# A row maximum that skips NaN: the last 34 tiles divided anew

## The chip, the cores and the metric

The kernel runs on one core of a Trainium2 chip. The metric is the device time of one execution in microseconds. A profile is one such execution, recorded by the hardware profiler; its own times count from the program's first instruction.

## The reference

```python
batch, seq, dim = 32, 2048, 2048
x = np.random.randn(batch, seq, dim).astype(np.float32)
x[np.random.rand(batch, seq, dim) < 0.1] = np.nan
...
return np.nanmax(x, axis=-1).astype(np.float32)
```

There are 65,536 rows of 2048 numbers, 537 MB, a tenth of them NaN. Of each row the largest number that isn't NaN is wanted; a row with nothing but NaN gives NaN.

## The kernel before, in words

**The tiles.** The rows lie on 128 partitions, 512 rows to each. The list `TILES` cuts them into 74 tiles, numbered here from 1. Its unit is the quarter: a quarter of a row, 512 elements of each partition. A tile of 28 quarters is seven rows of each partition, 7168 KB. An entry of `TILES` has three lists, each with the same sum:

- the loads: `[28]` is one DMA, `[20, 8]` are two;
- the pieces in which the tile is cleaned;
- the reductions: `[16, 12]` are four rows and then three.

**Cleaning a piece.** A NaN would spoil a maximum, so only the upper 16 bits of each number are treated. ACT (ScalarE) reads them and writes a "key" into a key buffer, with an activation whose two slopes send NaN to a low value (L222, `kt<-xt`). Then the key goes back, turned round, in place of the upper 16 bits. GpSimd does that (POOL, L232, `xt<-kt`) for a positive number in the list of pieces, and ACT does it (a "write-back", L222, `xt<-kt`) for a negative one. A tuple is one key operation whose parts go back separately, so `(9, -3)` is a key of 12 quarters of which GpSimd returns 9 and ACT 3. A write-back by ACT stands directly behind its key operation; one written as a float, `-3.0`, stands behind the next key operation. Then VectorE (DVE) takes the maximum over whole rows (L239).

**Buffers and order.** There are three tile buffers (`xt`), each 28 quarters, and three key buffers (`kt`), each 12. A tile's loads wait until the reductions of the tile three before it are done (L316). Loads are issued by SyncE (SP), in order. `Order` writes down all instructions and gives each the semaphore waits that it needs; every engine takes its own in the order in which they were written.

A key operation that doesn't fit into the rest of its key buffer goes to the next one and waits until what that one held has been returned. The last key operation of a tile waits for the buffer after that as well:

```python
if used + c > KEYS:
    key = (key + 1) % NKEYS
    used = 0
    kold, kfree[key] = last(kfree[key]), []
    ...
    if at + c == sum(loads) * Q:
        kold = kold + last(kfree[(key + 1) % NKEYS])
```

**Pairs.** Where a reduction needs one piece from GpSimd and one from ACT, and no other reduction needs either, `joints` makes them a pair: both count up one semaphore, and all who wait for either wait for both. That holds for the key buffers too: in `cleaned`, the event `e` with which a half's key buffer comes free is that of the pair.

```python
for a, b, k, back, when in both:
    kfree[k].append((back, when, e))
    clean.append((a, b, e))
```

`joints` leaves ACT's half out where GpSimd's piece belongs to a later step than the write-back. Tiles 70 to 73 (`APART`) have no pairs.

**The end.** Rows without a number are turned into NaN by a pass over the results (L245, twice, and L260 with L274 for one group on GpSimd), and six stores bring the results out (L461). The last store is issued when the last pass is done.

Of the kernel before, what the change touches and what calls it, by code (L numbers as in the profile page):

```python
# [23 lines left out]
    + [([28], [7, 9, 12], [16, 12])] * 7  # L24
    + [([28], [9, 12, -7], [8, 20])]
    + [([28], [7, 9, 12], [16, 12])] * 7
    + [([28], [9, 12, -7], [8, 20])]
    + [([28], [7, 9, 12], [16, 12])] * 7
    + [([28], [6, 10, 12], [16, 12])] * 3
    + [([28], [7, 9, 12], [16, 12])]  # L30
    + [([28], [6, 10, 12], [16, 12])] * 3
    + [([28], [7, 9, 12], [12, 16])] * 2
    + [([28], [7, 10, 11], [12, 16])]
    + [([28], [6, 10, 12], [16, 12])] * 3
    + [([28], [8, 11, 9], [8, 8, 12])]
    + [([20, 8], [11, -6, 6, 5], [16, 12])]
    + [([20, 8], [12, (-4, 7), 5], [8, 8, 12])]
    + [([17, 11], [12, (-4, 6), 6], [4, 12, 12])]
    + [([16, 12], [11, -5, 5, 7], [16, 12])]
    + [([13, 15], [9, -4, 7, 8], [12, 8, 8])]  # L40
    + [([14, 14], [9, -4, 4, 4, 7], [12, 8, 8])]
    + [([11, 10, 7], [5, 6, (-3, 7), 7], [4, 4, 4, 8, 8])]
    + [([11, 9, 8], [4, 7, (-2, 7), 6, -2], [4, 4, 4, 8, 8])]
    + [([8, 7, 6, 7], [3, 5, 7, (3, -3), 3, 4], [8, 4, 8, 8])]
    + [([6, 5, 6, 5, 6], [5, (5, -1), (-1, 5), 5, 3, 3], [4, 4, 4, 4, 4, 4, 4])]
    + [([5, 6, 5, 4, 4, 3, 1], [(-2, 3), 3, 3, (4, -1), 4, 4, -2.0, 2], [4, 4, 3, 1, 4, 4, 4, 4])]
    + [([4, 4, 3, 2, 4, 2, 3, 3, 3], [2, 2, 4, (-2.0, 1), 2, 3, 3, (-1, 2), (1, -1, 1), 2, -1.0], [4, 4, 4, 4, 4, 4, 4])]
)

GROUPS = [TILES[i : i + 15] for i in range(0, 60, 15)] + [TILES[60:73], TILES[73:]]  # L50
# [453 lines left out]
```

## Time and profile before

| | |
|---|---|
| median of 3 executions | 1252.54 us (1252.48 to 1253.04) |
| the profiled execution | 1252.48 us |
| its span | 1250.7 us |
| VectorE busy | 1111.4 us, 89% |
| ScalarE busy | 965.6 us, 77% |
| GpSimd busy | 1168.5 us, 93% |
| DMA, mean rate | 430 GB/s |

A line of the profile names the source line, the engine, the operation, what is written and read with partitions x elements, and how often; behind the bar are the busy time in us, the mean of one in ns, and the idle time before it with what ended it. "ACT kt L222" are key operations, "POOL xt L232" GpSimd's returns, "DVE acc L239" the reductions. In a timeline a line has its start and length in us, and a merged one counts its instructions (x3) and has the shape of the first.

### The profile page before, as it was taken

To read this page: it belongs to the slowest core of one execution; us is meant where nothing else is said; L and a number is where in the kernel's file an instruction comes from. 1 tells how busy PE (TensorE), PEld (TensorE's weight loads), DVE (VectorE), ACT (ScalarE), POOL (GpSimd) and SP (SyncE) were. 2 spreads that over 40 slices of the span, in tenths; PEclk is the share of its full clock that TensorE was granted. 3 is DMA by queue.
4 is the path that set the end of the run, shared out by engine and by line. 5 is a ranking of instruction groups with operands and counts; after the bars stand their busy time and mean duration, and the time that the engine had idled before them with its cause. 6 is when DMAs were issued, how large, how long until landed. Compare 5 with 4: busy or idle time off the path is not lost.

```text
span 1250.7 us, 891 instructions
## 1 busy us (share of the span) xinstructions
DVE 1111.4 (89%) x179; ACT 965.6 (77%) x273; POOL 1168.5 (93%) x242
## 2 busy tenths in 40 slices
DVE  0888989888889888898988888998888899999999
ACT  3777887778777877788777877777777778999997
POOL 2999989998999899998999899999999999989998
DMA  9999999999999999999999999999999999999997
GB/s 415 440 418 433 440 440 438 413 440 440 440 433 418 440 440 438 429 424 440 440 436 424 431 440 438 436 424 433 440 438 435 422 436 436 425 434 429 431 428 301
DMA packets 15991, 537.20 MB, mean 430 GB/s; under 512 B 2544, under 2 KB 2544, under 8 KB 3568
## 3 DMA queue, kind: packets, MB, share of 16 engines
q1 hardware_dynamic: 15984, 537.14, 99.4%
q14 instruction: 7, 0.06, 0.0%
HBM read 536.87 MB, written 0.26 MB: 429 GB/s over the span
## 4 chain that ended last, share of the span: by engine, by line
DMA 40%; DVE 29%; POOL 22%; ACT 9%; issue 1%; SPq 0%
DMA xt<-in_x_dram 40%; DVE acc L239 29%; POOL xt L232 22%; ACT kt L222 8%; ACT xt L222 1%; SPq L316 0%; DVE acc L245 0%; SPq L499 0%; SPq L215 0%
## 5 line engine op out<-in xcount | busy, mean ns | idle before, releaser
L232 POOL TENSOR_SCALAR xt<-kt 128x3584 int16<-128x3584 uint16 (+11 forms) x236 | 1167.4, 4947 | 77.6 <-ACT kt L222 63.9
L239 DVE TENSOR_REDUCE acc<-xt 128x3 f32<-128x6144 f32 (+4 forms) x175 | 1107.5, 6379 | 135.6 <-POOL xt L232 128.1
L222 ACT ACTIVATE kt<-xt 128x3584 uint16<-128x3584 int16 (+9 forms) x247 | 913.4, 3734 | 278.0 <-DMA xt<-in_x_dram 257.9
L222 ACT ACTIVATE xt<-kt 128x512 int16<-128x512 uint16 (+6 forms) x24 | 52.8, 2202 | 0.7
L245 DVE SCALAR_TENSOR_TENSOR acc<-acc 128x414 f32<-128x414 f32 (+1 forms) x2 | 2.2, 1111 | 0.1
L222 ACT ACT_TABLE_LOAD x1 | 1.3, 1283 | 0.9 <-SPq L215 0.9
L239 DVE TENSOR_REDUCE xt<-xt 128x1 f32<-128x1536 f32 x1 | 1.7, 1743 | 0.0
L278 DVE MEMSET scalars<- 128x1 f32 x1 | 0.1, 59 | 1.0 <-SPq L215 1.0
L260 POOL TENSOR_SCALAR late<-acc 128x91 int32<-128x91 f32 x1 | 0.5, 549 | 0.1
L274 POOL TENSOR_TENSOR acc<-acc,late 128x91 int32<-128x91 int32 x1 | 0.3, 341 | 0.1
L485 POOL MEMSET const-float32-0.0<- 128x1 f32 x1 | 0.1, 98 | 0.2 <-issue 0.2
L222 ACT ACTIVATE scalars<-scalars 128x1 f32<-128x1 f32 x1 | 0.2, 203 | 0.0
L485 POOL MEMSET const-bfloat16-1.0<- 128x1 bf16 x1 | 0.1, 101 | 0.0
L485 POOL MEMSET const-uint8-127<- 128x1 uint8 x1 | 0.1, 101 | 0.0
L485 POOL MEMSET const-float32-1.0<- 128x1 f32 x1 | 0.1, 98 | 0.0
## 6 DMA issues: line engine op xcount, KB each, us to landing
xt<-in_x_dram SPq DMA_DIRECT2D x61, 7168.0 KB, 22.6
xt<-in_x_dram SPq DMA_DIRECT2D x2, 5120.0 KB, 17.4
xt<-in_x_dram SPq DMA_DIRECT2D x3, 2816.0 KB, 22.7
xt<-in_x_dram SPq DMA_DIRECT2D x4, 2048.0 KB, 22.3
xt<-in_x_dram SPq DMA_DIRECT2D x5, 1536.0 KB, 29.1
xt<-in_x_dram SPq DMA_DIRECT2D x2, 3584.0 KB, 24.8
xt<-in_x_dram SPq DMA_DIRECT2D x6, 1024.0 KB, 26.8
xt<-in_x_dram SPq DMA_DIRECT2D x3, 1792.0 KB, 30.1
```

What stands on the lines that cost most here:

```text
L222: lambda: nc.scalar.activation(**kw),
L232: lambda: nc.gpsimd.tensor_scalar(**kw),
L239: return order.add("dve", nc.vector, lambda: do(**kw), deps)
L245: lambda: nc.vector.scalar_tensor_tensor(out=acc, in0=acc, scalar=LEAST, in1=acc, op0=ALU.is_ge, op1=ALU.mult,),
L260: lambda: nc.gpsimd.tensor_scalar(out=none, in0=acc, scalar1=LEAST, scalar2=float(0x00400000), op0=ALU.is_lt, op1=ALU.mult,),
L274: lambda: nc.gpsimd.tensor_tensor(out=bits, in0=bits, in1=none, op=ALU.add),
L278: e_warm = order.add("dve", nc.vector, lambda: nc.vector.memset(warm, 1.0), [])
L485: nc = _bacc.Bacc("TRN2", target_bir_lowering=False, num_devices=1)
```

## The change

Only `TILES` is changed, from the 41st entry on; tiles 53 and 61 stay as they were. In tiles 41 to 60 each tile is still one load, three pieces and two reductions, with other sizes, and ACT's one write-back among them, the 7 quarters of tile 41, goes to GpSimd. From tile 62 on, loads, pieces and reductions are cut otherwise. In all there are 116 loads (105 before), 246 key operations (247), 23 write-backs by ACT with 80 quarters (24 with 84), 241 returns by GpSimd (236) and 177 reductions of tiles (176).

```diff
-    + [([28], [9, 12, -7], [8, 20])]
-    + [([28], [7, 9, 12], [16, 12])] * 7
-    + [([28], [6, 10, 12], [16, 12])] * 3
-    + [([28], [7, 9, 12], [16, 12])]
-    + [([28], [6, 10, 12], [16, 12])] * 3
-    + [([28], [7, 9, 12], [12, 16])] * 2
+    + [([28], [8, 9, 11], [16, 12])]
+    + [([28], [7, 11, 10], [16, 12])]
+    + [([28], [8, 9, 11], [12, 16])]
+    + [([28], [9, 8, 11], [12, 16])] * 2
...
+    + [([28], [8, 9, 11], [12, 16])]
+    + [([28], [6, 11, 11], [16, 12])]
     + [([28], [7, 10, 11], [12, 16])]
-    + [([28], [6, 10, 12], [16, 12])] * 3
-    + [([28], [8, 11, 9], [8, 8, 12])]
-    + [([20, 8], [11, -6, 6, 5], [16, 12])]
-    + [([20, 8], [12, (-4, 7), 5], [8, 8, 12])]
-    + [([17, 11], [12, (-4, 6), 6], [4, 12, 12])]
-    + [([16, 12], [11, -5, 5, 7], [16, 12])]
-    + [([13, 15], [9, -4, 7, 8], [12, 8, 8])]
-    + [([14, 14], [9, -4, 4, 4, 7], [12, 8, 8])]
-    + [([11, 10, 7], [5, 6, (-3, 7), 7], [4, 4, 4, 8, 8])]
-    + [([11, 9, 8], [4, 7, (-2, 7), 6, -2], [4, 4, 4, 8, 8])]
-    + [([8, 7, 6, 7], [3, 5, 7, (3, -3), 3, 4], [8, 4, 8, 8])]
-    + [([6, 5, 6, 5, 6], [5, (5, -1), (-1, 5), 5, 3, 3], [4, 4, 4, 4, 4, 4, 4])]
-    + [([5, 6, 5, 4, 4, 3, 1], [(-2, 3), 3, 3, (4, -1), 4, 4, -2.0, 2], [4, 4, 3, 1, 4, 4, 4, 4])]
-    + [([4, 4, 3, 2, 4, 2, 3, 3, 3], [2, 2, 4, (-2.0, 1), 2, 3, 3, (-1, 2), (1, -1, 1), 2, -1.0], [4, 4, 4, 4, 4, 4, 4])]
+    + [([28], [6, 10, 12], [16, 12])]
+    + [([28], [8, (5, -7.0), 8], [12, 16])]
+    + [([28], [5, 7, 9, 7], [12, 8, 8])]
+    + [([20, 8], [(7, -5.0), 8, 8], [12, 8, 8])]
+    + [([15, 13], [(9, -3.0), 8, 8], [8, 8, 12])]
+    + [([13, 15], [(9, -3), 8, 8], [8, 12, 8])]
+    + [([15, 13], [10, -4, 6, 8], [12, 8, 8])]
+    + [([14, 14], [9, (-3, 2), 7, 7], [12, 8, 8])]
+    + [([11, 6, 11], [(6, -5.0), (3, 3), 4, 7], [4, 8, 8, 8])]
+    + [([9, 9, 10], [(7, -2), (6, -3), 3, 2, 5], [8, 8, 4, 8])]
+    + [([8, 7, 6, 7], [7, -1, 7, (3, -3), 3, 4], [8, 4, 8, 8])]
+    + [([7, 4, 6, 4, 7], [5, (5, -1), (2, 4), (-3, 1), 2, 3, 2], [4, 4, 4, 8, 4, 4])]
+    + [([5, 6, 5, 1, 1, 1, 2, 1, 1, 1, 1, 1, 1, 1], [(-1, 4), 3, 3, (-1, 4), 3, 4, 3, -2.0], [4, 4, 4, 4, 3, 1, 3, 1, 4])]
+    + [([4, 4, 3, 2, 2, 1, 1, 2, 2, 1, 2, 1, 1, 2], [2, 2, 4, 3, -2, 1, 2, 3, (1, 2), (-1, 2), (-2, 1)], [4, 4, 4, 4, 3, 1, 2, 2, 4])]
```

The last minus line and the last plus line are tile 74, and each line above it is one tile earlier, up to tile 61 (`[6, 10, 12]`). In the new tile 65, `[(9, -3.0), 8, 8]` with `[8, 8, 12]`, the second reduction covers quarters 8 to 16: the end of GpSimd's 9, ACT's 3 and the start of GpSimd's first 8.

## The prediction

> **What bounds the kernel now.** I read the busy shares first, then DMA and VectorE (DVE) by stretches of time, then DVE's timeline, and last ACT's and POOL's where the changed tiles begin. Tiles are counted from 1, and a quarter is 512 elements of a partition.
>
> ```profile
> span 1250.7 us, 891 instructions
> DVE 1111.4 (89%) x179; ACT 965.6 (77%) x273; POOL 1168.5 (93%) x242
> 850.00:1000.00 150.00, 134.62 (x18) 111.57 (x27) 146.72 (x27) 1.00 1.00 434
> 1050.00:1100.00 50.00, 49.84 (x10) 47.61 (x15) 47.90 (x11) 1.00 1.01 435
> 1100.00:1150.00 50.00, 49.88 (x9) 47.53 (x18) 43.70 (x11) 1.00 1.00 431
> 1150.00:1200.00 50.00, 50.00 (x16) 45.53 (x20) 48.76 (x16) 1.00 1.00 430
> 1200.00:1251.00 51.00, 48.04 (x24) 42.67 (x33) 43.86 (x26) 1.00 0.84 348
> ```
>
> The stretches give DVE, ACT and POOL busy time, clock, DMA share and GB/s. DMA is full until the last stretch: a tile of 28 quarters takes 16.9 us of it, whatever the engines do. DVE needs about 15.2 us for such a tile, so up to 1000 us it waits (134.62 of 150 busy). After 1050 us it doesn't: 49.84, 49.88 and 50.00 of 50. There a second bound stands beside DMA: DVE has a fixed amount of reducing left and no idle time in which to make good a stop.
>
> ```profile
> 1017.40 15.15 DVE L239 TENSOR_REDUCE acc<-xt 128x4 f32<-128x8192 f32 x2 [1.74 <-POOL xt L232]
> 1034.56 23.79 DVE L239 TENSOR_REDUCE acc<-xt 128x4 f32<-128x8192 f32 x4
> 1058.51 60.52 DVE L239 TENSOR_REDUCE acc<-xt 128x3 f32<-128x6144 f32 x10 [0.16 <-POOL xt L232]
> 1065.07 45.38 DVE acc L239 x8
> 1247.94 0.17 DVE acc L245
> ```
>
> Three lines are DVE's timeline, two the chain that ended last. DVE's last wait of any size ends at 1017.40 (tile 60). The chain's eight reductions from 1065.07 end at 1110.46, and the eighth is the last of tile 65: 12 quarters, 6.54 us, begun at 1103.92. From there to the end of the reductions at 1247.94 are 144.0 us, the time to which the change is compared.
>
> ```profile
> 1038.03 19.98 ACT L222 ACTIVATE kt<-xt 128x4096 uint16<-128x4096 int16 x5 [4.48 <-DMA xt<-in_x_dram]
> 1065.06 7.55 ACT L222 ACTIVATE kt<-xt 128x2560 uint16<-128x2560 int16 x2 [0.79 <-POOL xt L232]
> 1072.70 14.44 POOL L232 TENSOR_SCALAR xt<-kt 128x6144 int16<-128x6144 uint16 x3 [0.83 <-ACT kt L222]
> ```
>
> At 1038.03 ACT starts tile 62 as its load lands; earlier waits of this kind end at 1004.26 and 1021.14, so the bytes of tile 63 are there at 1038.03 + 16.9 = 1054.93. The other two lines show, small, what I expect large. The last key operation of tile 63 waits 0.79 us for POOL, because a tile's last key asks for the next key buffer as well, and a buffer whose pieces are a "pair" comes free only when both halves are done. POOL then runs dry for 0.83 us. DVE didn't feel it: pieces lay ready for it.
>
> **The change part by part.** Durations are the means by shape.
>
> ```profile
> L232 POOL TENSOR_SCALAR xt<-kt 128x4608 int16<-128x4608 uint16 x53 | 282.8, 5335 | 9.1 <-ACT kt L222 5.4
> L232 POOL TENSOR_SCALAR xt<-kt 128x3584 int16<-128x3584 uint16 x55 | 230.7, 4194 | 44.5 <-ACT kt L222 43.1
> L232 POOL TENSOR_SCALAR xt<-kt 128x2560 int16<-128x2560 uint16 x9 | 27.4, 3049 | 2.1 <-ACT kt L222 1.6
> L232 POOL TENSOR_SCALAR xt<-kt 128x4096 int16<-128x4096 uint16 x2 | 9.5, 4762 | 0.3 <-ACT kt L222 0.2
> L222 ACT ACTIVATE kt<-xt 128x4096 uint16<-128x4096 int16 x2 | 7.2, 3609 | 4.5 <-DMA xt<-in_x_dram 4.5
> L222 ACT ACTIVATE kt<-xt 128x2560 uint16<-128x2560 int16 x10 | 23.2, 2325 | 1.3 <-POOL xt L232 0.8 <-DMA xt<-in_x_dram 0.5
> ```
>
> *Tiles 41 to 60.* ACT's one write-back of 7 quarters (4.20 us) becomes POOL's. POOL's share of a tile is then 4.19 + 5.34 + 7.04 + 3 x 0.08 = 16.81 us of 16.9, so a backlog is worked off by 0.1 us a tile. Carried through POOL's pieces, tile 60's first reduction starts near 1018.2, 0.8 us later than now. The bounds are 0 and 4.2; I take 0.8. It sets only how late DVE comes to the next step, not the end.
>
> *Tile 65, the step that decides.* Its pieces are now (9, -3.0), 8, 8 with reductions of 8, 8 and 12. The second reduction needs ACT's -3 and POOL's first 8, so `joints` makes these two a pair, and the key buffer that holds the -3 is free only when POOL has done that 8. The tile's last key waits for this buffer. So it stands on ACT until POOL has written all it has been given, and POOL has nothing meanwhile. In tile 63 of before POOL still had a piece in hand.
>
> The time: tile 63 lands at 1054.93; ACT's first key (5 quarters) ends at 1057.28, POOL starts at 1057.35 and then has 5, 7, 9, 7 (tile 63), 7, 8, 8 (tile 64), 9, 8 (tile 65) in a row: 3.05 + 4.19 + 5.34 + 4.19 + 4.19 + 4.76 + 4.76 + 5.34 + 4.76 = 40.58, eight handovers of 0.08, and 0.1 where ACT's key for tile 65 is late: 41.32, to 1098.67. Then the waiting key, 0.02 + 3.61, to 1102.30; POOL's last 8, 0.07 + 4.76, to 1107.13; DVE starts the last reduction of tile 65 at 1107.15. Now it starts at 1103.92: 3.23 us later. ACT waits 4.3 us (its write-back of 3 quarters is done near 1094.3), POOL 3.7. Queued behind the key on ACT are the keys of tile 66, for which POOL waits too.
>
> DVE itself: the reductions of tiles 61 to 64 are the same, and tile 65's are 8, 8, 12 for 4, 12, 12, which sums the same. With its 0.8 us it would be ready near 1104.4, so 2.7 us of the stop show as idle.
>
> *Reducing left.* In tiles 66 to 74, 44 reductions become 45: sixteen of 8 quarters (4.41), three of 12 (6.54), eighteen of 4 (2.28), three of 1536 elements (1.74), three of 513 (0.69), two near 1024 (1.2, between the last two): 140.8 us, against 140.7. With tile 65's last 6.54, less 0.08 of overlap at 41 handovers, plus 0.02 at the four that wait for DVE's own result: 144.0 us, as now. ACT and POOL stay ahead of it: in the tail POOL finishes each piece some 2.8 us before DVE asks for it. There are two thin places, the reductions near 1118 and 1129, with 0.1 us to spare; their bounds are 0 and 0.3 us, and I take 0.
>
> *Eleven more loads* (105 to 116): one fewer in tile 63, seven more in 73, five in 74. SP issues one in 0.43 us by the chain; the stores stand behind them on SP, which is free at the latest when the last load lands, and the last store is due near 1251.4. Between 1150 and 1200 eleven loads land, between 850 and 1000 three in 50 us; the rate goes from 434 to 430 GB/s, 0.46 us in 50 for eight more, about 0.05 us a load: the last landing, at 1242.2 in the trace's DMA records, comes 0.5 us later (bounds 0 and 0.1 us a load). It is hidden: everything behind the stop has 2.7 us more between landing and reduction. Without the stop it would show.
>
> The Trainium skill speaks against this part: DMA: Bandwidth & Descriptors, section Rules for kernel authors, asks for 1 MiB or more per DMA and for coalescing small transfers. Its section on the anatomy of one DMA has a fixed part of about 2.0 us each (for the GpSimd path), by which eleven would cost 22 us, an estimate from that page.
>
> *The sum.* 1107.15 + 144.0 = 1251.15; the flagging pass and the last store as now (1250.7 - 1247.94 = 2.76) give a span of 1253.9, 3.2 more. The profiled execution took 1252.48, its span and 1.78 around it, and the median is 0.06 above that: 1253.9 + 1.84 = 1255.8.
>
> **The rivals.** *The stop doesn't reach DVE* (12%). In tile 63 of before the same kind of wait cost DVE nothing. It would do so here if DVE came to tile 65's last piece 2.7 us later, or POOL 2.7 us earlier, than I have it. DVE is then 0.5 us behind before: 1253.0, not measurably slower. Against it: POOL's row of nine pieces starts from a landing, and their durations spread by hundredths. Parts of the stop would give 1253 to 1255.
>
> *Loads that pay one by one* (5%). The stores that met an empty queue took this from issue to landing:
>
> ```profile
> out_dram<-acc SPq DMA_DIRECT2D x1, 3.5 KB, 1.4
> ```
>
> If each added load held the stream for 1.4 us, the last landing would come 15.4 later and the end with it: 1268. From 2.7 us in all (0.25 us a load) it would begin to show. Against it: 430 GB/s while those eleven landed in 50 us. By the rule on small transfers the time would go this way; the trace doesn't agree so far, with 0.05 us for a load.
>
> *Faster* (2%). The smaller last pieces shorten the way from the last landing to the end, now 5.7 us. But DVE has had under half a microsecond of idle time since 1017, and its reducing is not less; over 2.5 us are not to be had.
>
> That the sharing hardly changes is so: ACT's write-backs go from 24 to 23 (84 to 80 quarters), POOL's pieces from 236 to 241.
>
> **How the numbers follow.** My case has 81%. A measurement can tell about 0.2% here, 2.5 us, so slower begins at 1255.05 and my 1255.8 is close above it. Around it I allow 0.8 us: 0.3 for the landing of tile 63, 0.3 for the thin places, and the 0.5 by which the runs of before differ. The range reaches down into the partly hidden stop and up to a tail that loses a microsecond: 1254.2 to 1257.0. Slower takes nearly all of my case and the 5%: 0.82. The hidden stop and my case's lower edge give no change: 0.15. Faster: 0.03.
>
> **What would show it.** Right: one ACT key of 4096 elements near 1098.7 that waits about 4.3 us for POOL, a POOL piece near 1102.4 that waits 3.7 for ACT, a reduction near 1107.2 that waits 2.7 for POOL, and hardly any idle time of DVE after it; the last landing near 1242.7. Wrong: DVE idle under 1 us there, DVE waits after 1120 us, or DMA below 425 GB/s between 1150 and 1230.

## The result, and the profile after

The changed kernel takes 1255.99 us (median of 8, 1255.89 to 1256.43), the kernel before 1252.45 (median of 8): 1.0028 times as long, 95% interval 1.0018 to 1.0039. It was forecast at 1255.8, with a range from 1254.2 to 1257.0.

The profiled execution took 1255.89 us. From its page, and from its answer by stretches of time (DVE, ACT, POOL busy, clock, DMA share, GB/s):

```profile
span 1254.1 us, 918 instructions
DVE 1111.6 (89%) x180; ACT 963.2 (77%) x271; POOL 1171.7 (93%) x247
1050.00:1100.00 50.00, 50.00 (x10) 44.22 (x14) 45.37 (x10) 1.00 0.99 428
1100.00:1150.00 50.00, 46.87 (x9) 48.71 (x16) 46.47 (x11) 1.00 1.00 431
1150.00:1200.00 50.00, 50.00 (x14) 48.04 (x22) 47.57 (x17) 1.00 1.00 429
```

The engines' totals hardly moved: DVE is up by 0.2 us, POOL up by 3.2, ACT down by 2.4. By themselves they don't say where a span that is 3.4 us longer comes from. The stretches say where to look: from 1100 to 1150 DVE was busy for 46.87 us, where it had been 49.88. In the stretch that follows it is full again, so what was lost there was not won back.

The timelines of ACT, POOL and DVE in that place, one line or two of each:

```profile
1054.88 9.35 ACT L233 ACTIVATE kt<-xt 128x2560 uint16<-128x2560 int16 x3 [0.47 <-DMA xt<-in_x_dram]
1092.36 1.90 ACT L233 ACTIVATE xt<-kt 128x1536 int16<-128x1536 uint16 x1
1098.66 8.83 ACT L233 ACTIVATE kt<-xt 128x4096 uint16<-128x4096 int16 x2 [4.40 <-POOL xt L243]
1088.46 10.17 POOL L243 TENSOR_SCALAR xt<-kt 128x4608 int16<-128x4608 uint16 x2 [0.17 <-ACT kt L233]
1102.36 4.76 POOL L243 TENSOR_SCALAR xt<-kt 128x4096 int16<-128x4096 uint16 x1 [3.73 <-ACT kt L233]
1107.15 121.47 DVE L250 TENSOR_REDUCE acc<-xt 128x3 f32<-128x6144 f32 x32 [3.13 <-POOL xt L243]
1251.35 0.17 DVE L256 SCALAR_TENSOR_TENSOR acc<-acc 128x7 f32<-128x7 f32 x1
```

Read them as a relay. ACT's write-back of 3 quarters is done at 1094.26 (1092.36 + 1.90). Its next instruction, the last key of tile 65, waits 4.40 us, until POOL's two pieces that began at 1088.46 are written at 1098.63. POOL has now nothing to do for 3.73 us, about as long as ACT needs for that key (3.63 us in the chain below). DVE, ready at 1104.02, waits 3.13 us for POOL's piece. From 1107.15 to the last pass at 1251.35 it has no further gap over 0.04 us.

The chain that ended last shows the same handovers:

```profile
1093.89 4.75 POOL xt L243
1098.66 3.63 ACT kt L233
1102.29 0.07 issue
1102.36 4.77 POOL xt L243
1107.15 64.22 DVE acc L250 x14
```

### The profile page after: what moved, and what is told of

It reads as the page before. It is cut to its first block, busy times and chain, and to the rows that moved or that the text cites. A ratio compares the mean times of both kernels' runs of the same rounds, so it can differ in the third digit from the quotient of the medians.

```text
span 1254.1 us, 918 instructions
## 1 busy us (share of the span) xinstructions
DVE 1111.6 (89%) x180; ACT 963.2 (77%) x271; POOL 1171.7 (93%) x247
## 4 chain that ended last, share of the span: by engine, by line
DMA 35%; DVE 33%; POOL 19%; ACT 11%; issue 2%; SPq 0%
DMA xt<-in_x_dram 35%; DVE acc L250 32%; POOL xt L243 19%; ACT kt L233 10%; ACT xt L233 1%; DVE xt L250 1%; SPq L327 0%; DVE acc L256 0%; SPq L510 0%; SPq L226 0%
## 5 line engine op out<-in xcount | busy, mean ns | idle before, releaser
L250 DVE TENSOR_REDUCE acc<-xt 128x3 f32<-128x6144 f32 (+5 forms) x173 | 1104.0, 6427 | 138.8 <-POOL xt L243 132.4
L233 ACT ACTIVATE kt<-xt 128x3584 uint16<-128x3584 int16 (+11 forms) x246 | 913.2, 3748 | 281.6 <-DMA xt<-in_x_dram 244.1
L233 ACT ACTIVATE xt<-kt 128x1536 int16<-128x1536 uint16 (+5 forms) x23 | 50.3, 2189 | 0.6
L250 DVE TENSOR_REDUCE xt<-xt 128x1 f32<-128x1536 f32 (+1 forms) x4 | 6.4, 1611 | 0.0
```

The source lines that it names most:

```text
L233: lambda: nc.scalar.activation(**kw),
L250: return order.add("dve", nc.vector, lambda: do(**kw), deps)
```

## The experiments

Theory S is the forecast's: the pair of tile 65 makes its last key wait until POOL has an empty hand, the stop reaches DVE, and DVE can't make it good. Theory L blames the eleven added loads, theory M the larger share of GpSimd in tiles 41 to 60. In these runs the kernel before had a median of 1252.5 us each time.

**Without the pair**

```diff
-APART = (70, 71, 72, 73)
+APART = (65, 70, 71, 72, 73)
```

> The changed kernel with tile 65 among those without pairs; nothing else differs. Theory S (the pair of tile 65 stops ACT, then POOL, then VectorE): the 4.4 us wait of ACT near 1094, POOL's 3.7 and VectorE's 3.1 at 1104 are gone; VectorE's reductions end near 1248.7 (1251.35 with the pair) and the time is 1253.2, about 0.7 above before: what stays is a tail whose data come about as late as VectorE asks for them. Theory L (the eleven added loads cost the time): nothing changes, 1256.0. Theory M (GpSimd's larger share in tiles 41 to 60 cost it): 1256.0 too, with VectorE idle elsewhere.

1253.16 us (11 runs), 1.0006 times before (0.9997 to 1.0015). ACT and POOL in that place, and DVE from there on:

```profile
1094.34 8.83 ACT L233 ACTIVATE kt<-xt 128x4096 uint16<-128x4096 int16 x2
1088.56 20.47 POOL L243 TENSOR_SCALAR xt<-kt 128x4608 int16<-128x4608 uint16 x4 [0.18 <-ACT kt L233]
1034.85 190.82 DVE L250 TENSOR_REDUCE acc<-xt 128x4 f32<-128x8192 f32 x44
```

The key of 4096 elements starts at 1094.34, directly behind the write-back. POOL's four pieces follow one another, and DVE's 44 reductions from 1034.85 are one line without idle time. One number in a tuple, with no size and no load changed, takes 2.8 of the 3.5 us away.

**The same, by another way**

```diff
-    + [([15, 13], [(9, -3.0), 8, 8], [8, 8, 12])]
+    + [([15, 13], [(9, -3), 8, 8], [8, 8, 12])]
```

> The changed kernel with ACT's write-back of tile 65 as -3 in place of -3.0: it stands directly behind its key, a step before POOL's first 8, so no pair is made; all sizes stay. Theory S: as without the pair, 1253.2, no wait of ACT over 1 us between 1090 and 1104 and VectorE without a gap. Rival (the cutting 9, 3, 8, 8 itself is what costs): 1256.

1253.63 us (11 runs), 1.0008 times before (0.9999 to 1.0017), 0.4 above what was expected. ACT, POOL and DVE:

```profile
1090.71 12.53 ACT L233 ACTIVATE kt<-xt 128x4096 uint16<-128x4096 int16 x3
1088.98 20.43 POOL L243 TENSOR_SCALAR xt<-kt 128x4608 int16<-128x4608 uint16 x4 [0.18 <-ACT kt L233]
1050.45 71.27 DVE L250 TENSOR_REDUCE acc<-xt 128x3 f32<-128x6144 f32 x13
```

The wait is gone here too, and so is the gap near 1104; behind it DVE has only two small ones, of 0.19 and 0.12 us. So it is the pair, and not that the tile is cut in 9, 3, 8 and 8. In the profile tile 63 landed 0.43 us later than without the pair (1055.40 for 1054.97), and from there to the last pass are 193.60 us for 193.46, so most of what lies above the expectation in that execution is the landing.

**The pieces of tile 65 in the kernel before**

```diff
-    + [([17, 11], [12, (-4, 6), 6], [4, 12, 12])]
+    + [([17, 11], [(9, -3.0), 8, 8], [8, 8, 12])]
```

> The kernel before with the pieces and reductions of tile 65 alone from the changed one, (9, -3.0), 8, 8 and 8, 8, 12; loads and all other tiles as before. Theory S: the stop comes with these pieces: ACT waits 3 to 4.5 us for POOL before the tile's last key, VectorE is idle 2.3 us or more near 1106, its reductions end near 1250.2 for 1247.9, and the time is 1254.7, 2.2 above before. Theories L and M: 1252.5.

1254.75 us (11 runs), 1.0018 times before (1.0009 to 1.0027). ACT, POOL and DVE:

```profile
1098.14 10.63 ACT L222 ACTIVATE kt<-xt 128x4096 uint16<-128x4096 int16 x3 [3.44 <-POOL xt L232]
1101.84 11.31 POOL L232 TENSOR_SCALAR xt<-kt 128x4096 int16<-128x4096 uint16 x2 [3.73 <-ACT kt L222]
1106.64 117.30 DVE L239 TENSOR_REDUCE acc<-xt 128x3 f32<-128x6144 f32 x32 [2.30 <-POOL xt L232]
```

One line of the change, put into the kernel before, brings the stop and 2.25 us. It is less than the 3.5 us of the whole change. In the two profiles (1255.01 and 1255.89 us) DVE goes on at 1106.64 for 1107.15 in the changed kernel, 0.51 us earlier, and needs 143.83 us for 144.20 from there to the last pass. The rest of the 1.2 us between the medians lies within the spread of the executions.

**Something in POOL's hand, and a longer stop**

Two kernels keep the pair and alter what stands behind it. In the first the last 8 quarters are two pieces of 4, so that POOL has one of them while ACT waits and makes the last key. In the second the last two pieces are 4 and 12.

```diff
-    + [([15, 13], [(9, -3.0), 8, 8], [8, 8, 12])]
+    + [([15, 13], [(9, -3.0), 8, 4, 4], [8, 8, 12])]   # the first
+    + [([15, 13], [(9, -3.0), 4, 12], [8, 8, 12])]     # the second
```

> The changed kernel with tile 65's last 8 quarters cut in 4 and 4: the pair stays, ACT still waits for POOL's paired piece before the tile's last key, but POOL has one piece of 4 quarters (2.48 us) in hand meanwhile. Theory S (what costs is POOL's empty hand, the last key's and the last piece's time one behind the other): ACT waits about 2.6 us near 1096, POOL 2.1 near 1104 for 3.7, VectorE 0.5 near 1116 for 3.1; the reductions end near 1249.6 and the time is 1254.2, 1.8 below the changed kernel and 0.9 above the one without the pair. Rival (the pair's wait itself costs, whatever POOL has in hand): 1255.5 to 1256.

> The changed kernel with the last two pieces of tile 65 as 4 and 12 in place of 8 and 8: the same pair, but the key that waits is 12 quarters (5.32 us) and POOL's piece behind it as well (7.04 us); the wait begins earlier, since POOL's paired piece is 2.48 us in place of 4.76. Theory S: POOL idle 5.4 us near 1102, VectorE 4.2 to 4.8 near 1109, the reductions end near 1253.1, and the time is 1257.7. Rival (the pair's wait itself costs): ACT waits 3.9 us for 4.4 before, so 1255.5.

The first takes 1254.43 us (11 runs), 1.0016 times before (1.0007 to 1.0025); the second 1258.11 (5 runs), 1.0046 (1.0033 to 1.0058). The start of tile 63 on ACT as its load lands, then ACT, POOL and DVE at the stop, then the last pass, of the first and of the second:

```profile
1054.86 9.35 ACT L233 ACTIVATE kt<-xt 128x2560 uint16<-128x2560 int16 x3 [0.47 <-DMA xt<-in_x_dram]
1098.64 7.12 ACT L233 ACTIVATE kt<-xt 128x2048 uint16<-128x2048 int16 x2 [2.67 <-POOL xt L243]
1105.84 10.18 POOL L243 TENSOR_SCALAR xt<-kt 128x4608 int16<-128x4608 uint16 x2 [2.12 <-ACT kt L233]
1111.21 4.42 DVE L250 TENSOR_REDUCE acc<-xt 128x2 f32<-128x4096 f32 x1 [0.76 <-POOL xt L243]
1116.05 6.55 DVE L250 TENSOR_REDUCE acc<-xt 128x3 f32<-128x6144 f32 x1 [0.43 <-POOL xt L243]
1249.50 0.17 DVE L256 SCALAR_TENSOR_TENSOR acc<-acc 128x7 f32<-128x7 f32 x1
```

```profile
1055.88 9.35 ACT L233 ACTIVATE kt<-xt 128x2560 uint16<-128x2560 int16 x3 [0.52 <-DMA xt<-in_x_dram]
1097.37 10.54 ACT L233 ACTIVATE kt<-xt 128x6144 uint16<-128x6144 int16 x2 [3.80 <-POOL xt L243]
1102.77 17.29 POOL L243 TENSOR_SCALAR xt<-kt 128x6144 int16<-128x6144 uint16 x3 [5.44 <-ACT kt L233]
1109.84 10.88 DVE L250 TENSOR_REDUCE acc<-xt 128x3 f32<-128x6144 f32 x2 [4.88 <-POOL xt L243]
1254.03 0.17 DVE L256 SCALAR_TENSOR_TENSOR acc<-acc 128x7 f32<-128x7 f32 x1
```

ACT waits less in the second (3.80 us) than in the changed kernel (4.40), and the kernel is 2.1 us slower. So the length of ACT's wait isn't the price. What counts is how long POOL stands empty behind it and how long the piece is that DVE then needs: 2.12, 3.73 and 5.44 us of idle POOL go with 1.19, 3.13 and 4.88 us of idle DVE and with 1254.4, 1256.0 and 1258.1 us. Counted from the landing of tile 63, which came 1.0 us later in the second profile, to the last pass, the three kernels take 194.64, 196.47 and 198.15 us: steps of 1.83 and 1.68 us for 1.61 and 1.71 us more of idle POOL. The first kernel had a second small gap of DVE, at 1111.21, which was not expected.

**Tiles 41 to 60 alone**

The kernel before with tiles 41 to 60 of the changed one; all from 61 on as before.

> The kernel before with tiles 41 to 60 of the changed one; all from 61 on as before. Theory S: no stop, VectorE's last wait ends near 1018.2 for 1017.4, and of these 0.8 us about 0.3 are left at the end: 1252.8 (bounds 1252.4 and 1253.3). Theory M: most of the loss is here, 1255 to 1256. Theory L: 1252.5.

1252.79 us (11 runs), 1.0002 times before (0.9994 to 1.0011): not to be told from no change. Theory M falls. In the profile DVE's last wait of any size ended at 1019.01, 0.8 us later than expected; the loads were 1.0 us late by then, against the kernel before (see the last section).

**The loads, put in and taken out**

The loads of tiles 73 and 74, twelve more in the kernel before, twelve fewer in the changed one; their pieces and reductions stay in both.

```diff
-    + [([5, 6, 5, 4, 4, 3, 1], ...
-    + [([4, 4, 3, 2, 4, 2, 3, 3, 3], ...
+    + [([5, 6, 5, 1, 1, 1, 2, 1, 1, 1, 1, 1, 1, 1], ...
+    + [([4, 4, 3, 2, 2, 1, 1, 2, 2, 1, 2, 1, 1, 2], ...
```

> The kernel before with the loads of tiles 73 and 74 alone from the changed one: twelve more, pieces and reductions as before. Theory S: a load costs the stream 0.045 us, the last landing comes 0.5 us later (1242.7 for 1242.2), and without 2.7 us of cover a part of it shows: 1252.7 (bounds 1252.4 and 1253.1). Theory L: most of the loss is here, 0.25 us a load or more, 1255.5 or above, with gaps in the stream of loads near the end.

> The changed kernel with the loads of tiles 73 and 74 of the kernel before, twelve fewer; pieces and reductions stay. Theory S: the last landing comes 0.5 us earlier, and nothing else, since behind the stop the data lie ready some 2.7 us before VectorE asks: 1256.0 as the changed kernel, within 0.2. Theory L (loads cost the time): 1253 or below 1255.3.

Put into the kernel before: 1252.86 us (11 runs), 1.0002 times (0.9993 to 1.0011). Taken out of the changed kernel: 1256.61 (5 runs), 1.0032 (1.0019 to 1.0045), so not faster either, and 0.6 above what was expected. For the profiled execution, which took 1256.94, the trace says why. ACT's start of tile 63, DVE's start behind the stop, and its last pass:

```profile
1055.97 9.35 ACT L233 ACTIVATE kt<-xt 128x2560 uint16<-128x2560 int16 x3 [0.48 <-DMA xt<-in_x_dram]
1108.21 10.88 DVE L250 TENSOR_REDUCE acc<-xt 128x3 f32<-128x6144 f32 x2 [3.13 <-POOL xt L243]
1252.40 0.17 DVE L256 SCALAR_TENSOR_TENSOR acc<-acc 128x7 f32<-128x7 f32 x1
```

In this execution tile 63 landed 1.09 us later than in the profile of the changed kernel (1055.97 for 1054.88). From there to the last pass are 196.43 us, and 196.47 with the twelve loads. So in these two profiles the loads behind the stop are worth nothing; the other executions of this kernel have no trace. Theory L falls.

## Why the prediction was right, point by point

- **The stop.** The chain of steps was forecast as 1098.67 for the end of POOL's row of pieces, 1102.37 for the start of its last piece, 1107.15 for DVE; it was 1098.63, 1102.36 and 1107.15. Each is a row's mean duration behind a landing, on engines with a fixed order, and the two experiments without the pair take the stop away. That it fits to hundredths is in part luck: in the six profiles with the changed tiles 41 to 64, tile 63 landed between 1054.86 and 1055.97, where the forecast had allowed 0.3 us around 1054.93.
- **No second bound.** 144.0 us of reducing were forecast behind the stop; from 1107.15 to 1251.35 are 144.2. The forecast's own terms add up to 144.1 (140.8 + 6.54 - 41 x 0.08 + 4 x 0.02), a slip that changes nothing. The two places with 0.1 us to spare cost nothing.
- **DVE's idle time.** 2.7 us were forecast, it was 3.13. Tile 60's first reduction began at 1018.22, as worked out, but the flagging pass behind tile 60 took 1.33 us in place of 2.06. DVE came to the stop 0.4 us earlier than forecast, at 1104.02, and waited longer. The end isn't touched, since the stop ends when POOL is done. This is why such a sum should start from the engine that ends the wait.
- **The loads.** 0.05 us for each was forecast, and a last landing near 1242.7. In the DMA records it is at 1242.24 before and at 1243.18 after. Counted from the mean end of tile 61's packets it comes after 229.45 to 229.99 us in the three profiles with the loads of before, and after 230.01 to 230.48 in the five with those of the changed kernel. The means, 229.72 and 230.23, are 0.5 us apart, about 0.05 for each of eleven; the spread is as large, so two profiles alone can't tell (before and after alone give 0.76). With twelve loads added it is 230.20, with twelve taken out 229.70. That is inside the bounds, and the cover held. The Trainium skill's 2.0 us a DMA (page DMA: Bandwidth & Descriptors, section Anatomy of one DMA — SWDGE (gpsimd) path) are for DMAs issued by GpSimd. The loads here are issued by SP and queue behind others, and the 22 us that the forecast worked out from that figure don't show. One term of the forecast held only in part: 0.43 us is SP's median for an issue between 1150 and 1200 in the kernel before, but behind that a single issue took up to 9.54 us (5.16 before). The last store still went out at 1251.5, right behind the last pass.
- **The rival in which the stop doesn't reach DVE** gave 1253.0; without the pair it is 1253.16. What the rest of the change costs is then 0.7 us, within what a measurement can tell. The expectation for the kernel without the pair put this down to a tail whose data come about as late as DVE asks for them. Its profile shows something else: from tile 60's first reduction on DVE is never idle for more than 0.09 us, so its own work sets the end. That reduction begins at 1018.32 for 1017.40 before, 0.92 us later, of which the stream of loads accounts for 0.21 (the mean end of tile 61's packets); from there to the last pass are 230.11 us for 230.54, with a flagging pass that is 0.73 us shorter. How the 0.7 us between the medians divide between the middle and the loads is left open, since each alone is within 0.4 us of nothing.

## What to carry to other kernels

Where an engine has no idle time left until the end, look not at its share but for the one wait that it can't absorb, and follow the engine that ends this wait back to a landing. A shared semaphore that frees a buffer only when both of two engines are done can turn a harmless wait into a stop, if the second engine gets its next work from the one that waits. The price here was about the time for which that engine stood empty. A small piece left in its hand gave back 1.6 of the 3.5 us, and undoing the pair 2.8.

## What the runs showed of the hardware that was not expected

The stream of loads isn't quite the same in every execution. In ten profiles whose tiles up to 61 are loaded alike, one DMA for each of the tiles 2 to 61, the mean end of tile 61's packets lay between 1012.52 and 1013.64 us. The stream slips by some tenths of a microsecond at one tile or another, and stays late. In the kernel with fewer loads, against the kernel before, it slipped by 0.2 between tiles 6 and 11, by 0.4 between 11 and 21, by 0.25 between 41 and 51 and by 0.3 between 51 and 61. A kernel whose end hangs on a landing takes this over to the full, as the profile of that kernel shows; why the stream slips is open.

The first flagging pass, one DVE instruction on the same 414 numbers a partition, takes 2.06 or 2.07 us in the three profiled kernels with tile 60 of before, and 1.32 to 1.34 in the seven with the changed one. Before, then after:

```profile
1032.58 2.06 DVE L245 SCALAR_TENSOR_TENSOR acc<-acc 128x414 f32<-128x414 f32 x1
1033.49 1.33 DVE L256 SCALAR_TENSOR_TENSOR acc<-acc 128x414 f32<-128x414 f32 x1
```

The runs don't tell why.
